# Seven products of quarters for the input projection of a hybrid state-space and attention layer

## The chip, the cores and the metric

The kernel runs on one core of one Trainium2 chip. The metric is the device time of one execution in microseconds; less is better.

## The reference

One transformer-like layer, in float32, over 1024 tokens of a prompt and 64 tokens of a second sequence that has a past of 512 tokens and stored states. Cut to what matters:

```python
xn = _rmsnorm(x, p['norm_mix_w'])
proj = xn @ p['w_in']                     # 1024 x 9248
z, xbc, dt_raw, q, k, v, gate_ssm, gate_att = jnp.split(proj, ...)   # 2048, 3072, 32, 1024, 1024, 1024, 1024, 1024
xbc_c = jax.nn.silu(causal_dwconv(conv_past, xbc, ...))              # 4 taps
y_ssm = rmsnorm_by_group(ssd_scan(...) * jax.nn.silu(z))             # 4 groups of 8 heads
q = _partial_rope(_rmsnorm(q, p['q_norm_w']), q_pos)                 # 16 heads of 64
k = _partial_rope(_rmsnorm(k, p['k_norm_w']), q_pos)
o = _rmsnorm(_diff_attention(q, k_all, v_all, q_pos, k_pos, lam))    # softmax 0 - lam * softmax 1, chunked mask
mix = sigmoid(gate_ssm) * (y_ssm @ p['w_branch_ssm']) + sigmoid(gate_att) * (o @ p['w_branch_attn'])
x = x + mix @ p['w_out']
h = _rmsnorm(x, p['norm_ffn_w']) @ p['w_up']
x = x + (silu(conv3(ha)) * hb) @ p['w_down']
```

## The kernel before

All 1088 tokens lie along the free dimension (T = 1088, HT = 544 is a half). Features lie on the 128 partitions, so the 1024 inputs are KT = 8 tiles. Every float32 operand is split into a high part, rounded to the format in which TensorE multiplies (written fp32r in the profile's rows), and the rest, its low part; `product` multiplies high by high, high by low and low by high, three matmuls a tile of the contraction.

`project(block, evac)` makes one 128-column block of w_in: it loads and splits the block (`weights`, L150 to L152: a DMA, a ScalarE copy, a VectorE subtraction), then runs 8 x 3 matmuls for each of the three column chunks of WIDE = 384, 384, 320 tokens (L158 to L160) and hands each to `evac`.

The stages, in the order of time:
- The first two quarters of the values, from plain rows while the norm's roots are computed (`plain_rows`, `token_roots`, `values`).
- `heads` for q, and for k: eight blocks each, squares, the norm, the rotation of a part, and the split rows written to q_st and k_st. The other two quarters of the values lie between (`values(2, ...)`, `values(3, ...)`).
- Attention: 8 heads of 9 units (`attend`), a unit being 128 queries. A unit's first half makes two score tiles, their maxima, exponentials and the difference of both; its second half transposes the difference and multiplies with the values. The loop runs the second half of a unit after the first half of the next one. After each unit, `fill(ATT_STEPS)` takes 1.66 steps of a stream of `project` chunks: 16 blocks z, 24 convolution blocks, 16 gate blocks (ORDER). 17 steps stand ahead (FIRST).
- The scan of the state-space part, beside it the rest of the stream and two of three `branch` products (1.5 steps at each yield), then the third branch.
- `output`, then the up projection and the down projection, both by seven products: `left_parts` makes the seven left operands from the four quarters of a pair of weight blocks, B and `right_parts` hold the right ones, and `pair`, `down_pair` run 7 x 2 steps, each 4 x 3 matmuls of QW = 272 columns (L1227, L1390), and add up the quadrants.

The names in the rows: xn is the normed input, w_hi, w_lo and wh split weights, sc the scores, p_t the exponentials, a_t and po the transposed differences and the output of a unit, pt their PSUM tile, cc and pre the convolution's rows, ye (L871) the state's products.

The order of instructions on each engine is that of the program, with `high_priority` moving loads and evacuations up, settled by a planner that gives each a due time. PSUM has eight banks: `acc` goes round the banks of `pm` and of a stage's own pool (`more`).

Of the kernel before, what the change touches and what calls it, by code (L numbers as in the profile page):

```python
# [17 lines left out]
P = 128  # L18
# [5 lines left out]
WIDE = ((0, 384), (384, 384), (768, 320))  # L24
EPS = 1e-6
# [22 lines left out]
QR = 10  # L48
QSQ = 1
# [3 lines left out]
XR = 5  # L53
ROOTS = ((0, 1), (1, 3), (3, 6), (6, 9))
QUICK = 400
AT = 4
AHEAD_IN = 100
# [3 lines left out]
FIRST = 17  # L61
ATT_STEPS = 1.66
# [4 lines left out]
def group(g):  # L67
    return 16 + g, 20 + g, *range(4 * g, 4 * g + 4)


ORDER = (("g", (15, 14)), ("z", range(4)), ("c", group(0)), ("g", range(13, 7, -1)), ("c", group(1)), ("c", group(2)),
         ("z", range(4, 8)), ("c", group(3)), ("z", range(8, 16)), ("g", range(7, 1, -1)))

# [7 lines left out]
def hybrid_layer(ctx: ExitStack, tc: tile.TileContext, xT, xt, prm, cst, rope, wvd, win, wbs, wba, wout, wup, wdn,  # L81
# [12 lines left out]
    q_st, k_st = (scratch(n, [2 * D, T]) for n in ("q_st", "k_st"))  # L94
    c_st = scratch("c_st", [2 * D, PAST])
    m_sc, n_sc = scratch("m_sc", [D, T]), scratch("n_sc", [D, T])
# [30 lines left out]
    xn_pool = tc.alloc_tile_pool(name="xn", bufs=1, side="right")  # L127

    def rows_by_part(name):

        return [[xn_pool.tile([P, KT, w], R32, name=f"{name}_{u}{x}", tag=f"{u}{x}") for u in ("hi", "lo")]
                for x, (c, w) in enumerate(WIDE)]

    xn = rows_by_part("xn")
# [26 lines left out]

    def project(block, evac):
        w_hi, w_lo = weights(block, KT, P)
        for (c, w), (hi, lo) in zip(WIDE, xn):
            ps = acc(w)
            product(ps, [(w_hi[:, k], w_lo[:, k], hi[:, k], lo[:, k]) for k in range(KT)])
            with tc.high_priority(quick or ahead):
                evac(ps, c, w)
            yield

    def branch(stage, side, src, wts, gates, adds, out, step=1):

        parts = rows_by_part("b")
# [10 lines left out]
        if gates is not None and not adds:  # L184
            ready = {(m, c): next_to(m, c, w) for c, w in WIDE for m in TURNS[0]}
        for (c, w), (hi, lo) in zip(WIDE, parts):
            for k in range(0, KT, step):
                if stage is None:
                    for u, t in enumerate((hi, lo)):
                        load(out=t[:, k : k + step].bitcast(F32),  # L190
                             in_=src[D * u + P * k : D * u + P * (k + step), c : c + w].rearrange("(k p) t -> p k t", p=P))
                else:
                    t = stage()[:, :w]
                    load(out=t, in_=src[P * k : P * (k + 1), c : c + w])
                    S.copy(hi[:, k], t)
                    V.tensor_tensor(out=lo[:, k], in0=t, in1=hi[:, k], op=ALU.subtract)
        for ms in TURNS:
            wt = [weights(wts[m], KT, P) for m in ms]
            for (c, w), (hi, lo) in zip(WIDE, parts):
                for m, (w_hi, w_lo) in zip(ms, wt):  # L200
# [5 lines left out]
                    product(ps, [(w_hi[:, k], w_lo[:, k], hi[:, k], lo[:, k]) for k in range(KT)])  # L206
# [11 lines left out]
                    yield  # L218
# [22 lines left out]
    conv_o = dq.tile([P, CONV_TILES, 6], F32, name="conv_o")  # L241

# [6 lines left out]
    def stat(w):  # L249
        t = ps1.tile([P, 512], F32, name="st", tag="st", bufs=3)  # L250
        return t[:, :w]

    st = tc.alloc_tile_pool(name="st", bufs=1, side="right")
# [3 lines left out]
    nx = tc.alloc_tile_pool(name="nx", bufs=1)  # L257
# [6 lines left out]
    def plain_rows():  # L264
        c = 0
        for x, w in enumerate(NORM):
            xc = nx.tile([P, KT, max(NORM)], F32, name="xc", tag="xc", bufs=3)
# [28 lines left out]
    def value_weights(f):  # L296
        return [weights(win[B_V + 2 * f - 4 + u], 4, 256) for u in range(2)]

    def values(f, w2, dt=None):
        m = 256 if dt is None else 272  # L300
        for i in range(9):
# [3 lines left out]
            product(ps, [(hi[:, k], lo[:, k],  # L305
                          w2[k // 4][0][:, k % 4], w2[k // 4][1][:, k % 4]) for k in range(KT)])
            vo = staged("vo")[:, :256]
            with tc.high_priority(quick or ahead):
                if dt is None:
                    S.copy(vo[:n], ps[:, :256])  # L310
                else:
                    act(vo[:n], ps[:, :256], AF.Copy, scale=rtok[:n, i : i + 1])
# [21 lines left out]
    two = [values(0, [t[1:] for t in w2], dtw)]  # L334
# [8 lines left out]
    two.append(values(1, [weights(wvd[2 + u], 4, 272, p) for u, p in enumerate((extra, first))], dtw))  # L343
# [3 lines left out]
    for i in range(8):  # L347
        for u in two:
            next(u, None)
        if i == 3:  # L350
# [3 lines left out]
            for a, b, by in ((O_CW, O_SN, 0.5), (O_SN, O_D, -0.5), (O_QN, O_FW, -1.0)):  # L354
                V.tensor_scalar_mul(par[:, a:b], par[:, a:b], by)
# [5 lines left out]
    more = s1.enter_context(tc.tile_pool(name="psx", bufs=3, space=PSUM)), 3  # L361
    nx.release()
    first.release()
    extra.release()
    extra = None

    with tc.tile_pool(name="qk", bufs=1) as qk:
        rp = qk.tile([P, 2, T], F32, name="rp")
        load(out=rp, in_=rope)
        wq8 = qk.tile([P, 8], F32, name="wq8")  # L370
        V.tensor_scalar_mul(wq8, par[:, O_QN : O_QN + 8], 0.125)

        def row(name, w=T):
            t = qk.tile([P, T], F32, name=name, tag="qr", bufs=QR)
            return t[:, :w]


        rrow = qk.tile([P, T], F32, name="rrow")
        ps = stat(P)
        PE.matmul(ps[:9], rtok, ident, start=True, stop=True)  # L380
        rt = qk.tile([9, P], F32, name="rt")
        S.copy(rt, ps[:9])
        load(out=r_sc, in_=rt)
        load(out=rrow, in_=r_sc.rearrange("a b -> (a b)")[:T].unsqueeze(0).to_broadcast([P, T]))

        def rooted_rows():

            parts = rows_by_part("xn")
            for (c, w), (hi, lo) in zip(WIDE, parts):
                for k in range(KT):  # L390
                    x = qk.tile([P, 384], F32, name="xr", tag="xr", bufs=XR)[:, :w]
                    load(out=x, in_=xT[:, k, c : c + w])
                    V.tensor_tensor(out=x, in0=x, in1=rrow[:, c : c + w], op=ALU.mult)
                    act(hi[:, k], x, AF.Copy, scale=col(O_MIX + k))
                    V.scalar_tensor_tensor(lo[:, k], x, col(O_MIX + k), hi[:, k], ALU.mult, ALU.subtract)
            return parts

        def split_out(src, j, n, to):
            hi = qk.tile([P, T], R32, name="qh", tag="qh", bufs=2)[:, :n]
            lo = qk.tile([P, T], R32, name="ql", tag="ql", bufs=2)[:, :n]  # L400
            S.copy(hi, src)
            V.tensor_tensor(out=lo, in0=src, in1=hi, op=ALU.subtract)
            for u, t in enumerate((hi, lo)):
                load(out=to[D * u + P * j : D * u + P * (j + 1), :], in_=t.bitcast(F32))

        def heads(blk0, wcol, to, plain, root=None):
            nonlocal ahead
            ss = row("ss")
            rows = [row("qr") for _ in range(KT)]

            def block(j):
                r = rows[j]

                def evac(ps, c, w):
                    S.copy(r[:, c : c + w], ps)
                    if j == 0:
# [14 lines left out]
            for _ in WIDE:  # L431
                for u in tiles[KT - 2 :]:
                    next(u)
# [1137 lines left out]
```

## Time and profile before

| | us |
|---|---|
| median of 3 runs | 2448.9 (2448.25 to 2450.0) |
| the profiled execution | 2450.28 |
| its span in the trace | 2448.5 |
| TensorE busy | 2413.0 |
| VectorE busy | 1606.9 |
| ScalarE busy | 1166.9 |
| GpSimd busy | 584.3 |

A matmul's busy time in the profile overlaps that of the next one, so busy TensorE says that it had work, and the distance of matmul starts says at what rate. The weight load ahead of each matmul has rows of its own, named PEld. Rows of groups have: line, engine, operation, output and inputs, shapes, count | busy us, mean ns of one | idle time of the engine before them and what ended it. Rows of the timeline have: start us, duration us, engine, line, operation, and a count where several of one line were merged.

### The profile page before, as it was taken

The page shows a single profiled execution, that of the slowest core. Times are in us where ns is not written, and L with a number is a line of the kernel's source. Part 1 is how long each engine was busy: PE and PEld are TensorE (multiplying, and loading weights), DVE is VectorE, ACT ScalarE, POOL GpSimd, SP SyncE. Part 2 cuts the span into 40 slices and gives each one's busy share as a digit, 9 for nine tenths or more (in the row PEclk, how much of TensorE's full clock was granted, in tenths as well). Part 3 has the DMA queues.
Part 4 walks back from the last instruction along what each step waited for, and adds up shares of the span by engine and source line. Part 5 has one row for each costly group of instructions (what it writes and reads, how often), then busy time and mean ns, then how long its engine had stood idle before and what let it go on. Part 6 is the DMA issues. An engine that isn't in the chain of part 4 may idle for free. (4 is left out here: it accounts for less than half of the span.)

```text
span 2448.5 us, 44118 instructions
## 1 busy us (share of the span) xinstructions
PE 2413.0 (99%) x16824; PEld 2334.3 (95%) x16824; DVE 1606.9 (66%) x2760; ACT 1166.9 (48%) x2517; POOL 584.3 (24%) x630
## 2 busy tenths in 40 slices
PE   8999999999999999999999999999999999998999
PEld 8999999999999999998899899999999999998999
DVE  4356366755878677538677664756977777786763
ACT  7244344644666455437655453434543343353541
POOL 0000000100111001005433341013255555535533
PEclk9999999999999999999999999999999999999999
DMA  7237368443543454264797864764124234268884
GB/s 251 94 106 258 102 247 251 146 142 109 167 142 121 131 167 125 76 208 161 256 322 259 294 218 147 224 209 154 56 91 173 91 134 163 79 240 222 203 215 79
DMA packets 245670, 418.31 MB, mean 171 GB/s; under 512 B 32137, under 2 KB 168466, under 8 KB 245330
## 3 DMA queue, kind: packets, MB, share of 16 engines
q1 hardware_dynamic: 238258, 402.40, 49.6%
q0 software_dynamic: 7200, 13.09, 3.6%
q8 instruction: 132, 2.16, 0.4%
q14 instruction: 80, 0.66, 0.1%
HBM read 277.38 MB, written 138.02 MB: 170 GB/s over the span
## 5 line engine op out<-in xcount | busy, mean ns | idle before, releaser
L158 PE MATMUL mm<-xn_hi,w_hi 128*128 128x384 f32 (+1 forms) x1408 | 471.2, 335 | 1.0 <-DVE zr L550 0.9
L160 PE MATMUL mm<-xn_hi,w_lo 128*128 128x384 f32 (+1 forms) x1408 | 467.8, 332 | 0.5 <-DVE w_lo L152 0.5
L159 PE MATMUL mm<-xn_lo,w_hi 128*128 128x384 f32 (+1 forms) x1408 | 467.1, 332 | 0.0
L158 PEld LDWEIGHTS mm<-xn_hi,w_hi 128*128 128x128 f32 x1408 | 264.7, 188 | 5.9 <-DVE zr L550 1.6
L160 PEld LDWEIGHTS mm<-xn_hi,w_lo 128*128 128x128 f32 x1408 | 264.6, 188 | 3.8 <-issue 2.0
L159 PEld LDWEIGHTS mm<-xn_lo,w_hi 128*128 128x128 f32 x1408 | 264.7, 188 | 3.0 <-issue 1.6
L152 DVE TENSOR_TENSOR w_lo<-w_f,w_hi 128x1024 fp32r<-128x1024 f32 (+1 forms) x114 | 143.6, 1260 | 111.9 <-ACT w_hi L151 109.4
L151 ACT CAST w_hi<-w_f 128x1024 fp32r<-128x1024 f32 (+1 forms) x114 | 119.6, 1050 | 113.5 <-PE mx L159 52.0
L1227 PE MATMUL mx<-n,wh 128*128 128x272 f32 x1128 | 150.5, 289 | 1.9 <-ACT wh L1042 1.2
L158 PE MATMUL mm<-b_hi,w_hi 128*128 128x384 f32 (+1 forms) x448 | 151.5, 339 | 0.9 <-ACT w_hi L151 0.5
L160 PE MATMUL mm<-b_hi,w_lo 128*128 128x384 f32 (+1 forms) x448 | 148.1, 331 | 0.3 <-DVE w_lo L152 0.3
L159 PE MATMUL mm<-b_lo,w_hi 128*128 128x384 f32 (+1 forms) x448 | 147.7, 330 | 0.1
L1227 PEld LDWEIGHTS mx<-n,wh 128*128 128x128 f32 x1128 | 144.9, 188 | 2.6 <-ACT wh L1042 1.4
L1227 PE MATMUL mx<-m,w_hi 128*128 128x272 f32 x752 | 143.8, 288 | 1.3 <-DVE hb L1263 1.1
L700 ACT ACTIVATE p_t<-sc,mx 128x1024 f32<-128x1024 f32 (+5 forms) x144 | 106.3, 741 | 80.8 <-DVE mx L691 38.3
L579 DVE SCALAR_TENSOR_TENSOR cc<-pre,par,cc 128x384 f32<-128x384 f32 (+1 forms) x216 | 125.6, 584 | 15.1 <-ACT cc L577 10.9
L1043 DVE TENSOR_TENSOR wh<-w_f,wh 128x512 fp32r<-128x512 f32 (+1 forms) x100 | 93.9, 941 | 40.9 <-ACT wh L1042 40.9
L1227 PEld LDWEIGHTS mx<-m,w_hi 128*128 128x128 f32 x752 | 118.2, 188 | 2.0 <-DVE hb L1263 1.5
L1244 POOL TENSOR_TENSOR hb<-hb,cc 128x544 f32<-128x544 f32 (+2 forms) x66 | 91.0, 1393 | 108.7 <-ACT w_hi L1042 61.1
L565 POOL MEMSET pre<- 128x3 f32 x24 | 2.4, 101 | 474.8 <-DMA z_sc<-zr 378.8
L1042 ACT CAST w_hi<-ws 128x512 fp32r<-128x512 f32 (+1 forms) x68 | 41.4, 608 | 150.3 <-PE mx L1227 82.6
L1227 PE MATMUL mx<-m,w_lo 128*128 128x272 f32 x376 | 108.3, 288 | 0.0
(418 smaller groups left out, 6513.6 us busy)
## 6 DMA issues: line engine op xcount, KB each, us to landing
w_f<-in_win_dram SPq DMA_DIRECT2D x76, 512.0 KB, 3.8
w_f<-in_wup_dram SPq DMA_DIRECT2D x45, 512.0 KB, 3.5
bc<-a_sc SPq DMA_DIRECT2D x32, 512.0 KB, 5.9
h_sc<-hb SPq DMA_DIRECT2D x44, 272.0 KB, 2.1
ht<-h_sc SPq DMA_DIRECT2D x22, 544.0 KB, 4.6
t_sc<-ht SPq DMA_DIRECT2D x22, 544.0 KB, 2.9
out_dram<-yq POOLq DMA_DIRECT2D x44, 272.0 KB, 5.6
x_sc<-cc SPq DMA_DIRECT2D x48, 192.0 KB, 2.4
```

Source lines behind the costliest of these rows:

```text
L151: S.copy(hi, w)
L152: V.tensor_tensor(out=lo, in0=w, in1=hi, op=ALU.subtract)
L158: PE.matmul(ps, a_hi, b_hi, start=i == 0, stop=False)
L159: PE.matmul(ps, a_hi, b_lo, start=False, stop=False)
L160: PE.matmul(ps, a_lo, b_hi, start=False, stop=i == n - 1)
L565: G.memset(pre[:, 0:3], 0.0)
L579: V.scalar_tensor_tensor(cc[:, :m], pre[:, i : i + m], cw(i), cc[:, :m], ALU.mult, ALU.add)
L700: act(p_t[:n, :nk], sc[c][:n, :nk], AF.Exp, bias=mx[:n, c : c + 1], accum_out=dst)
L1042: S.copy(hi, src)
L1043: V.tensor_tensor(out=lo, in0=src, in1=hi, op=ALU.subtract)
L1227: PE.matmul(ps, w[x][:, c], b[y][:, k], start=start and k == i == 0, stop=k == 3 and i == 2, skip_group_check=not start)
L1244: G.tensor_tensor(out=hb[h][:, o : o + n], in0=hb[h][:, o : o + n], in1=cc[:, d : d + n], op=ALU.mult)
```

## The change

The products for q, k, the convolution and 12 of the 16 z blocks leave `heads` and the stream and get a stage of their own, ahead of attention. It takes two blocks at a time: the pair's weights are four quarters (two halves of the contraction by two blocks), the tokens' rows four quarters (two halves of the contraction by two halves of the tokens), and seven products of quarters make the four quadrants, as the up projection does. INPUT has 26 pairs: 4 of q, 4 of k, then six times two of convolution and one of z.

- The right operands are made once. `rooted(k)` loads two rows of x, multiplies them by the norm's weight and root, forms t1 to t4, splits b11, b21 and t2 in place, and writes t3, t1, t4, b22 and b12 to scratch (p_sc); `load_part` loads and splits them before the stage, b12 at its end. The rows b11, b12, b21, b22 are then what `project` and the branches' buffers use.
- All four quarters of the values come first; `rooted` and `steps` lie beside the third and fourth.
- A half of the tokens, 544, is cut into columns of 384 and 160 (W2). `in_pair` runs, for each of seven products p and each cut s, `pile`: 4 x 3 matmuls. After each second step one left operand of the next pair is made (`left_parts`, its sums on GpSimd from the third pair on).
- The convolution is done for halves of the tokens, in `in_pair`, with the Silu function in place of a tanh and a VectorE step; z as well for these 12 blocks. Norm and rotation of q and k (`finishing`) go beside later pairs, by way of scratch (q_r, k_r); so do the cached keys.
- `project` and `branch` go over CH, four chunks of 384, 160, 384 and 160 tokens, in place of WIDE.
- The stream holds 20 blocks: 16 gates and 4 of z. `fill` counts by columns (363 are one), 0.45 a unit of attention, 4 ahead of it.
- In attention the second half of a unit runs after the first half of the second unit after it (DEEP = 2), with 5 buffers p_t for 4.

```diff
+W2, O2 = (384, 160), (0, 384)
+CH = tuple((HT * c + O2[s], W2[s]) for c in range(2) for s in range(2))
+UNIT = 363.0
+DEEP = 2
+PROBS = 5
-FIRST = 17
-ATT_STEPS = 1.66
+FIRST = 4
+ATT_STEPS = 0.45
+ORDER = (("g", (15, 14)), ("z", range(4 * ZS, 16)), ("g", range(13, 7, -1)), ("g", range(7, 1, -1)))
+INPUT = ([(k, i) for k in "qk" for i in range(4)]
+         + [x for i in range(2 * ZS) for x in (("c", 2 * i), ("c", 2 * i + 1), ("z", i))])
...
     def project(block, evac):
         w_hi, w_lo = weights(block, KT, P)
-        for (c, w), (hi, lo) in zip(WIDE, xn):
+        for (c, w), rows_of in zip(CH, plain):
...
+        def pile(key, p, s, start):
+            if start:
+                banks[key, s] = acc(W2[s])
+            ps, w, b = banks[key, s], left[n][p], parts[PARTS[p], s]
+            for k in range(4):
+                c = slice(P * k, P * (k + 1))
+                for i, (x, y) in enumerate(((0, 0), (0, 1), (1, 0))):
+                    PE.matmul(ps, w[x][:, c], b[y][:, k], start=start and k == i == 0, stop=k == 3 and i == 2,
+                              skip_group_check=not start)
+            return ps
...
+        def conv(r, c):
...
+            cc = row("fc", "cc")
+            act(cc[:, :n], pre[:, :n], AF.Identity, bias=col(O_CB + f), scale=cw(0))
+            for i in range(1, 4):
+                V.scalar_tensor_tensor(cc[:, :n], pre[:, i : i + n], cw(i), cc[:, :n], ALU.mult, ALU.add)
+            act(cc[:, :n], cc[:, :n], AF.Silu)
...
+    for n in range(1, len(INPUT)):
+        coming = in_parts(n + 1) if n + 1 < len(INPUT) else iter(())
+        u = pairs[1] if n == 1 else begun_in(n)
+        for at, (p, s) in enumerate(rest if n == 1 else [(p, s) for p in range(7) for s in range(2)]):
+            u.send((p, s))
+            if s == 1:
+                more_left(n + 1)
+            if at % 2 == 0:
+                next(beside, None)
...
+        if n in (3, 7):
+            beside = chain(beside, finishing("q" if n == 3 else "k"))
...
     def fill(rate):
         nonlocal spare
         spare += rate
-        while spare >= 1:
-            next(filler, None)
-            spare -= 1
+        while spare > 0:
+            w = next(filler, None)
+            if w is None:
+                break
+            spare -= w / UNIT
...
+                waiting.append((unit, done))
+                settle(DEEP)
                 fill(ATT_STEPS)
```

More of the change, by code (lines that the diff above doesn't have):

```diff
@@ L205, in branch @@
                     ps = acc(w)
[L206 removed]
+                    product_over(ps, w_hi, w_lo, rows_of)
                     with tc.high_priority(ahead):
@@ new lines, in hybrid_layer @@
+    making = chain(*(rooted(k) for k in range(4)))
+    for u in chain(third, fourth):
+        next(making, None)
+    run(making)
+    steps()
+    wq8 = cp.tile([P, 8], F32, name="wq8")
+    V.tensor_scalar_mul(wq8, par[:, O_QN : O_QN + 8], 0.125)
+    ahead = AHEAD
+    raw.release()
+    st.release()
+    rr.release()
+    xn_pool.release()
+    un2 = tc.alloc_tile_pool(name="xd", bufs=1)
+    rows_l = tc.alloc_tile_pool(name="rl", bufs=1)
+    rows_r = tc.alloc_tile_pool(name="rg", bufs=1, side="right")
```

671 lines of the change are left out of this document (392 added, 279 removed).

## The prediction

> **What bounds the kernel now.** I read the page's first part, then the busy time by stretch, then TensorE's timeline at three places, and last the groups by line of the engines that the change loads more.
>
> ```profile
> PE 2413.0 (99%) x16824; PEld 2334.3 (95%) x16824; DVE 1606.9 (66%) x2760; ACT 1166.9 (48%) x2517; POOL 584.3 (24%) x630
> ...
> 50.00:340.00 290.00, 288.84 (x1881) 283.75 (x1881) 136.80 (x209) 114.85 (x218) 0.00 (x0) 1.00 0.41 138
> 340.00:1080.00 740.00, 738.35 (x4732) 713.19 (x4731) 500.54 (x1060) 394.80 (x962) 48.60 (x144) 1.00 0.49 153
> ...
> 1720.00:2180.00 460.00, 456.32 (x3616) 453.80 (x3615) 349.03 (x535) 187.61 (x336) 230.05 (x251) 1.00 0.34 119
> ```
>
> In the stretch rows the columns are length, then busy time of PE, PEld (the weight loads), DVE, ACT and POOL, the granted clock, the share of the DMA engines and GB/s. TensorE is busy to 99.6% in the q, k stage (50 to 340 us), to 99.8% in attention (340 to 1080) and to 99.2% in the up projection, all at the full clock. Every other engine has room. A busy PE is not yet a PE at its peak, so the next thing to read is how far apart the matmuls start.
>
> ```profile
> 300.01 0.33 PE L159 MATMUL mm<-xn_lo,w_hi 128*128 128x384 f32 x1
> 300.19 0.33 PE L160 MATMUL mm<-xn_hi,w_lo 128*128 128x384 f32 x1
> 300.36 0.33 PE L158 MATMUL mm<-xn_hi,w_hi 128*128 128x384 f32 x1
> 300.53 0.33 PE L159 MATMUL mm<-xn_lo,w_hi 128*128 128x384 f32 x1
> ...
> 475.44 0.31 PE L160 MATMUL mm<-xn_hi,w_lo 128*128 128x320 f32 x1
> 475.59 0.31 PE L158 MATMUL mm<-xn_hi,w_hi 128*128 128x320 f32 x1
> 475.74 0.31 PE L159 MATMUL mm<-xn_lo,w_hi 128*128 128x320 f32 x1
> 475.88 0.31 PE L160 MATMUL mm<-xn_hi,w_lo 128*128 128x320 f32 x1
> 476.03 0.22 PE L686 MATMUL sc<-kh,q 128*128 128x128 f32 x1
> 476.09 0.27 PE L687 MATMUL sc<-kl,q 128*128 128x128 f32 x1
> 476.20 0.27 PE L686 MATMUL sc<-kh,q 128*128 128x128 f32 x1
> 476.31 0.55 PE L734 MATMUL po<-v_t,a_t 128*128 128x128 f32 x3
> ```
>
> Starts of 384-column matmuls are (300.53 - 300.01) / 3 = 173.3 ns apart, those of 320 columns (475.88 - 475.44) / 3 = 146.7 ns. The difference, 26.7 ns for 64 columns, is 0.417 ns a column, and leaves 13.3 ns fixed. So TensorE streams columns with nothing between, and the time of this kernel is its matmuls times their prices. What changes the time is the number and the widths of the matmuls, as long as nothing else comes late.
>
> **The price of a narrow matmul.** The change cuts 544 columns into 384 and 160. No row here has 160 columns. By columns alone it would take 160 x 0.417 + 13.3 = 80 ns. The scores above have 128 columns (by columns alone 66.7 ns): the first is followed after 0.06 us, the next ones after 0.11 us each. The second row of numbers to read is that of the weight loads, one ahead of each matmul.
>
> ```profile
> 476.03 0.19 PEld L687 LDWEIGHTS sc<-kl,q 128*128 128x128 f32 x1
> 476.14 0.19 PEld L686 LDWEIGHTS sc<-kh,q 128*128 128x128 f32 x1
> 476.25 0.53 PEld L734 LDWEIGHTS po<-v_t,a_t 128*128 128x128 f32 x4
> ...
> 1176.17 0.52 PEld L871 LDWEIGHTS ye<-in,start 128*128 128x128 f32 x4
> ...
> L158 PEld LDWEIGHTS mm<-xn_hi,w_hi 128*128 128x128 f32 x1408 | 264.7, 188 | 5.9 <-DVE zr L550 1.6
> ...
> L158 PEld LDWEIGHTS mm<-w_hi,xn_hi 128*64 128x64 f32 x16 | 2.2, 135 | 0.0
> ```
>
> Loads follow each other at 0.11 us when the matmuls between are short: 476.03 to 476.14 to 476.25; the next three steps (0.53 - 0.19) / 3 = 0.113; at 1176.17 it is (0.52 - 0.19) / 3 = 0.11, and those matmuls (the state's, L871) stream only 64 columns. A load of 128 columns lasts 188 ns, one of 64 columns 135 ns: 53 ns for 64 columns, so 106 ns for 128 besides a latency of 82 ns that overlaps. One load runs ahead of the running matmul, not two: the first narrow matmul of a run is cheap since its follower's weights came during the wide one before it. So a matmul of a run costs the longer of its columns and its load. For 384 columns that is 173.3 ns, for 160 columns the load, 106 to 113 ns; I take 111. The lower end by rows would be 80, if loads were ahead of narrow ones too; nothing here shows that.
>
> The Trainium skill, page "TensorE: Matmul & The Clock Gate", section "LDWEIGHTS (loading the stationary operand)", gives a load as its columns divided by 1.2, in ns, whatever the contraction: 107 ns for 128 columns, which speaks against narrow products, and the 188 and 135 ns above agree with its slope. The same page, section "Back-to-back issue gap", has N / 2.4 + 2.5 ns for an isolated matmul, 69 ns for 160 columns; by that figure alone, an estimate from the page, 4296 narrow matmuls would take 180 us less than by 111 ns, and it says itself that this leaves out the weight load.
>
> **The change part by part.** *Products.* Before, a 128-column block of weights takes 24 matmuls (8 tiles of the contraction, three terms) for each of 384, 384 and 320 columns: 24 x (173.3 + 173.3 + 146.7) = 11.84 us. The change takes two blocks at once by seven products of quarters: 7 x 4 x 3 = 84 matmuls for each width, 84 x (173.3 + 111) = 23.88 us a pair. 52 blocks (8 q, 8 k, 24 convolution, 12 z) become 26 pairs: 620.9 us for 615.7 us, **+5.2 us**. An eighth of the columns is saved and all of it goes into the narrow half: `pile` runs twelve matmuls of 384 columns and then twelve of 160. (With 80 ns it would be 553.2, -62.5 us.)
>
> The seven-product stage that is there already has 272-column halves:
>
> ```profile
> 2307.12 10.53 PE mx L1390 x84
> ```
>
> that is 125.4 ns each, 250.8 for 544 columns against 284.3 for 384 and 160. That is where the gain goes.
>
> *The chunks of all that stays.* `project` and `branch` now go over CH, four chunks of 384, 160, 384, 160, where WIDE had three. 20 blocks stay in the stream (4 z, 16 gates) and 24 in the three branches. Each takes 24 x 2 x 284.3 = 13.65 us in place of 11.84: +1.81 us x 44 = **+79.5 us**. (With 80 ns, +0.32 x 44 = +14.1 us.) Values, `output` and the up and down projections keep their widths.
>
> *Filler.* Before, 72 attention units took 1.66 steps each of the stream, now 0.45 in units of 363 columns (4.55 us); FIRST falls from 17 to 4. TensorE's sum does not change by that, but its cover over attention does.
>
> ```profile
> L686 PEld LDWEIGHTS sc<-kh,q x208: 133/188/193, 393.2 to 1051.7; 128*128 128x128 f32 x96, 128*64 128x64 f32 x8
> ...
> L756 PEld LDWEIGHTS pt<-con,o_t x72: 134/139/143, 485.5 to 1079.5; 128*128 128x128 f32 x64, 64*128 64x128 f32 x8
> ...
> L691 DVE TENSOR_REDUCE mx<-sc 128x1 f32<-128x1024 f32 (+4 forms) x80 | 76.7, 963 | 19.8 <-PE sc L687 18.6
> L704 DVE SCALAR_TENSOR_TENSOR p_t<-p_t,sm 128x1024 f32<-128x1024 f32 (+8 forms) x72 | 58.8, 816 | 2.0
> L152 DVE TENSOR_TENSOR w_lo<-w_f,w_hi 128x1024 fp32r<-128x1024 f32 x42 | 51.1, 1218 | 23.3 <-ACT w_hi L151 20.9 <-PE po L734 2.3
> ...
> L722 DVE COPY a_t<-pt 128x512 f32<-128x512 f32 (+3 forms) x56 | 29.7, 530 | 12.8 <-PE pt L715 12.5
> L695 DVE TENSOR_REDUCE mx<-sc 128x2 f32<-128x256 f32 (+3 forms) x32 | 26.0, 813 | 0.4
> L755 DVE SCALAR_TENSOR_TENSOR o_t<-o_t,ors,wsub 128x128 f32<-128x128 f32 (+1 forms) x72 | 19.7, 346 | 0.2
> ...
> L703 DVE SCALAR_TENSOR_TENSOR sm<-sm,nlam,s 128x1 f32<-128x1 f32 (+1 forms) x72 | 15.6, 217 | 1.9
> L760 DVE TENSOR_TENSOR ol<-pt,oh 128x512 fp32r<-128x512 f32 (+1 forms) x23 | 12.2, 536 | 6.8 <-ACT zr L549 2.7 <-DMA o_sc<-oh 2.0 <-DMA o_sc<-ol 2.0
> L702 DVE RECIPROCAL sm<-sm 128x1 f32<-128x1 f32 (+1 forms) x72 | 11.5, 159 | 25.3 <-ACT p_t L700 25.1
> ```
>
> Attention runs from its first score at 393 to its last transposes at 1080 us. Of these 686 us, 72 x 1.66 steps of 3.95 us, 472 us, are filler, so its own matmuls take some 214 us. After: 214 + 72 x 0.45 x 4.55 = 214 + 147 = 361 us. VectorE's own work there is 76.7 + 58.8 + 29.7 + 26.0 + 19.7 + 15.6 + 12.2 + 11.5 = 250 us (the smallest rows left out), and 11 blocks of filler bring 11 splits of 1.22 us, 13 us: about 0.73 of 361 us, with the small rows perhaps 0.8; in the up projection it runs at 349 / 460 = 0.76 beside a full TensorE. So VectorE should keep pace, with more small waits since less filler lies between a unit's scores and its softmax. Running the second half two units late is the cover for those: nothing new waits, it only holds one more `p_t` (5 buffers for 4). I put **+10 us** for attention, between 0 and 30.
>
> *VectorE and the others in the new stage.*
>
> ```profile
> L1238 DVE SCALAR_TENSOR_TENSOR cc<-pre,par,cc 128x546 f32<-128x546 f32 (+1 forms) x69 | 64.1, 929 | 7.4 <-ACT cc L1236 6.2
> L1043 DVE TENSOR_TENSOR wh<-w_f,wh 128x512 fp32r<-128x512 f32 x51 | 52.8, 1035 | 26.3 <-ACT wh L1042 26.3
> L1043 DVE TENSOR_TENSOR w_lo<-w_f,w_hi 128x512 fp32r<-128x512 f32 x17 | 25.6, 1507 | 0.0
> L1043 DVE TENSOR_TENSOR w_lo<-ws,w_hi 128x512 fp32r<-128x512 f32 x34 | 24.9, 733 | 1.0
> L1043 DVE TENSOR_TENSOR wh<-ws,wh 128x512 fp32r<-128x512 f32 x18 | 20.3, 1128 | 23.5 <-ACT wh L1042 23.5
> L1265 DVE TENSOR_TENSOR hb<-mx,u 128x272 f32<-128x272 f32 x25 | 11.0, 439 | 14.7 <-PE mx L1227 13.6 <-issue 1.1
> ```
>
> These are 17 pairs of the up projection. Seven weight splits a pair: 123.6 / 17 = 7.3 us. Five products added out of PSUM in two pieces, 10 x 0.44 = 4.4 us. A convolution pair adds 2 blocks x 2 halves x 3 taps of some 544 columns, 12 x 0.93 = 11.1 us. Together 22.8 us of VectorE beside 23.9 us of TensorE; a z pair has 11.7. The norms and rotations of k (`finishing`) come on top while the first four convolution pairs run, some 30 us by the same prices (twelve half rows of a scale and a split at 0.9 + 0.7 us, and four rotations), against 4 x 23.9 - (3 x 22.8 + 11.7) = 15.5 us of room: **+10 us**, between 0 and 25, since seven PSUM banks let TensorE run only a few products ahead. GpSimd and ScalarE stay far below.
>
> *Transitions.* The loads of t3, t1, t4 and b22 wait for the last value product, and stand on SP's queue ahead of the weights of the third pair; TensorE has four products of two pairs and t2's, 5 x 3.41 = 17 us, before it needs t3. The first head's loads wait for the last pair's rows behind 4 units of gates, 18 us. `rooted`'s arithmetic lies under 18 value products. DMA share was 0.41, so the added 5.6 MB each way of differences and the q and k round trip have room. **+5 us**, between -5 and +15.
>
> Sum: 5.2 + 79.5 + 10 + 10 + 5 = +110 us. The profiled execution took 2450.28 us (span 2448.5), the median of the runs is 2448.9, 1.4 us below: 2450.3 + 110 - 1.4 = **2559 us**.
>
> **The rivals.**
> *A narrow matmul costs its columns.* Then 26 pairs save 62.5 us, the chunks cost 14.1 us, and with 25 us of waits (TensorE is shorter, VectorE's room less) the time is 2449 - 48 + 25 = 2426 us. For it: the first narrow score (0.06 us). Against: each one after it, and the 64-column ones. It decides below a price of some 86 ns: 4296 narrow matmuls (26 x 84 + 44 x 48) turn 1 ns into 4.3 us, so (48 - 25) / 4.3 = 5 ns above 80 the saving and the waits cancel. The isolated gap of the Trainium skill (page and section above) would make it so; the rows of loads do not bear it out. Chance 0.12, of which 0.09 lies beyond 0.2% faster, 0.01 within and 0.02 beyond it slower; 0.2% is about what a measurement of this kernel can tell from no change.
> *VectorE becomes the bound.* If it can hold no more than the 0.76 it has in the up projection, convolution pairs take 22.8 / 0.76 = 30 us, 12 x 6.1 = +73 us, and attention (250 + 13 + some 25 of small rows) / 0.76 = 379, +18 us: 2449 + 85 + 91 + 5 = 2630 us. Against it: in the up projection VectorE waits, it isn't the one waited for. Chance 0.17.
> *Under 256 columns the stream runs at half rate.* 128 columns in 111 ns are also two times 128 columns. Then 160 cost 2 x 160 x 0.417 + 5 = 138 ns (5 as 111 ns has over 2 x 128 x 0.417), +27 x 4.3 = +116: 2675 us. Against it: the first narrow score's 0.06 us. Chance 0.05.
>
> **How the numbers follow.** The forecast has 0.66. Its own range: at 106 ns, without waits, 2449 + 63 = 2512; at 113 with all upper waits (+70) 2449 + 93 + 70 = 2612. To hold 8 in 10 the range goes from 2515 to 2660, which takes in the VectorE case and leaves out the first rival and the third. Slower 0.66 + 0.17 + 0.05 + 0.02 = 0.90, same 0.01, faster 0.09.
>
> **What would show it.** In the timeline of the new stage, twelve 160-column matmuls start 111 ns apart and their weight loads too; 80 ns would be the first rival, 138 the third. The new stage lasts about 630 us, a gate block 13.6 us, attention about 370 us. VectorE as the bound would show as TensorE's idle time ended by VectorE, above some 60 us in the convolution pairs. A stall at the start of the new stage ended by a DMA into t3 or by a split would be a transition mis-sized. A time below 2500 us makes the price of the narrow matmul wrong.

## The result and the profile after

| | before | after |
|---|---|---|
| median of the runs, us | 2448.8 (2448.25 to 2450.0) | 2704.0 (2702.8 to 2708.4) |
| span of the profiled execution, us | 2448.5 | 2701.0 |
| TensorE busy, us | 2413.0 | 2568.8 |
| TensorE idle (span less busy), us | 35.5 | 132.2 |

After to before is 1.1045, with an interval of 1.1026 to 1.1064. The change costs 255 us where +110 was forecast, and the time is 44 us above the end of the range. The page of after has, in its first two parts:

```profile
PE 2568.8 (95%) x18504; PEld 2471.7 (92%) x18504; DVE 1785.9 (66%) x3080; ACT 1230.3 (46%) x2623; POOL 720.6 (27%) x702
...
PEclk9999998999999999888999999989999999999999
```

There are 18504 - 16824 = 1680 more matmuls, and that is exact: 26 x 168 - 52 x 72 = 624 in the pairs and 44 x 24 = 1056 in the chunks. The price is read in TensorE's timeline of the new stage (L600 is `pile` in `in_pair`):

```profile
610.36 0.51 PE L600 MATMUL mx<-t,w_hi 128*128 128x384 f32 x2
610.71 0.34 PE L600 MATMUL mx<-t,w_lo 128*128 128x384 f32 x1
610.88 0.35 PE L600 MATMUL mx<-t,w_hi 128*128 128x160 f32 x2
611.06 0.28 PE L600 MATMUL mx<-t,w_lo 128*128 128x160 f32 x1
...
611.40 0.27 PE L600 MATMUL mx<-t,w_lo 128*128 128x160 f32 x1
...
612.07 0.28 PE L600 MATMUL mx<-t,w_lo 128*128 128x160 f32 x1
```

From 611.06 to 612.07 lie nine starts of 160 columns: 112 ns each. The two of 384 columns from 610.36 to 610.71 take 175 ns each. Over the whole of 600 to 790 us, where TensorE never waits (row below), 1327 matmuls take 190.00 us: 286.4 ns for a wide and a narrow one, where 284.3 was put down. So the products cost nearly what the prediction put down, 94 us at this distance for 5.2 + 79.5 = 85. The other 168 us of the span are TensorE waiting (132.2 - 35.5 = 97 us more idle) and TensorE working slower than its price (2568.8 - 2413.0 - 85 = 71 us; 9 of them are these 2 ns a pair, and most of the rest is the halved clock of the last section). Where, the busy time by stretch tells (columns as in the prediction):

```profile
100.00:150.00 50.00, 39.08 (x265) 35.75 (x265) 38.77 (x63) 22.85 (x46) 0.00 (x0) 0.83 0.68 233
300.00:530.00 230.00, 201.82 (x1287) 196.68 (x1286) 170.63 (x286) 90.18 (x162) 62.07 (x72) 0.93 0.53 179
600.00:790.00 190.00, 190.00 (x1327) 190.00 (x1326) 133.52 (x215) 78.47 (x138) 61.48 (x90) 1.00 0.25 88
820.00:1100.00 280.00, 278.50 (x1965) 265.31 (x1964) 158.08 (x362) 134.94 (x374) 0.00 (x0) 1.00 0.51 156
1100.00:1240.00 140.00, 106.67 (x610) 88.21 (x608) 104.56 (x274) 83.76 (x246) 0.00 (x0) 0.84 0.44 132
1700.00:1800.00 100.00, 88.74 (x554) 82.13 (x554) 59.39 (x117) 43.88 (x99) 18.80 (x10) 0.90 0.52 158
```

TensorE has gaps in three kinds of place, and in each the granted clock falls too: while the new stage begins and k is finished beside its pairs (100 to 150, 300 to 530), in the second half of attention (1100 to 1240), and in the scan and its end (1700 to 1800). Between them (600 to 790, 820 to 1100) it is as full as before. No engine is full in the gaps: VectorE is at 0.74 to 0.78 in the first three stretches with gaps and at 0.70 in 600 to 790, where TensorE never waits.

To put a number on each stage I added up its matmuls, each at its distance of starts at full clock (173.3, 146.7, 126.7, 111 ns for 384, 320, 272, 160 columns, and so on for the small ones), and took the sum from the stage's length. What is left, us (with 384 and 160 columns it holds the 9 us by which their pair is dearer):

| lost in | before | after | e1_272 | e8_pace | e6_cover | e10_all |
|---|---|---|---|---|---|---|
| start to first score (new stage with it) | 17 | 77 | 96 | 56 | 85 | 52 |
| attention | 17 | 79 | 78 | 80 | 55 | 65 |
| scan to output | 5 | 47 | 40 | 39 | 45 | 62 |
| up and down | 18 | 21 | 23 | 21 | 18 | 20 |
| sum | 57 | 224 | 237 | 196 | 203 | 199 |

So the 168 us are +60, +62, +42 and +3. In the four runs below that leave the new stage untouched, its row is 84 to 88, against 77 in after; differences up to 10 us in it say nothing. What ended TensorE's waits in after, and VectorE's in 300 to 530 us (engine, line, releaser: us in total, times, longest):

```profile
PE sc L916 <- ACT p_t L930: 24.4, 17, 3.9
PE mm L600 <- DVE u L673: 8.5, 3, 4.4
PE mm L157 <- DVE w_lo L149: 8.1, 5, 3.5
PE mm L155 <- DVE b_g L223: 7.3, 4, 4.3
PE mx L600 <- DVE u L671: 7.1, 4, 3.4
PE mx L600 <- DVE pre L682: 6.5, 3, 3.1
```

```profile
DVE x L712 <- DMA x<-k_r: 18.3, 9, 3.8
...
DVE pre L682 <- DMA k_st<-x: 3.9, 3, 2.3
```

In attention a score waits for the exponentials that free its bank (L930). In the convolution pairs TensorE waits for VectorE, which evacuates PSUM (L671, L673, L682). But VectorE itself is held: next in its order stands a step of k's norm (L712), whose row of k has not landed yet, and an evacuation that could run stands behind it. One such place, on VectorE and on TensorE:

```profile
420.47 0.79 DVE L712 SCALAR_TENSOR_TENSOR x<-x,par,ss 128x544 f32<-128x544 f32 x1 [2.39 <-DMA x<-k_r]
421.17 0.32 DVE L671 TENSOR_TENSOR u<-mm,u 128x160 f32<-128x160 f32 x1
```

```profile
421.55 1.57 PE L600 MATMUL mm<-t,wh 128*128 128x160 f32 x12 [1.84 <-DVE u L671]
```

And the row that the evacuation writes (L682) is at times one that still goes out to k_st.

### The profile page after: what moved, and what is told of

It is laid out like the page before. It is cut to its first block, busy times and chain, and to the rows that moved or that the text cites. A ratio compares the mean times of both kernels' runs of the same rounds, so it can differ in the third digit from the quotient of the medians.

```text
span 2701.0 us, 48417 instructions
## 1 busy us (share of the span) xinstructions
PE 2568.8 (95%) x18504; PEld 2471.7 (92%) x18504; DVE 1785.9 (66%) x3080; ACT 1230.3 (46%) x2623; POOL 720.6 (27%) x702
## 5 line engine op out<-in xcount | busy, mean ns | idle before, releaser
L155 PE MATMUL mm<-b,w_hi 128*128 128x160 f32 (+1 forms) x1152 | 364.1, 317 | 12.4 <-DVE b_g L223 7.3
L157 PE MATMUL mm<-b,w_lo 128*128 128x160 f32 (+1 forms) x1152 | 361.0, 314 | 8.1 <-DVE w_lo L149 8.1
L156 PE MATMUL mm<-b,w_hi 128*128 128x160 f32 (+1 forms) x1152 | 360.5, 313 | 0.0
L155 PEld LDWEIGHTS mm<-b,w_hi 128*128 128x128 f32 x1152 | 223.8, 194 | 18.9 <-DVE b_g L223 6.2
L157 PEld LDWEIGHTS mm<-b,w_lo 128*128 128x128 f32 x1152 | 223.9, 194 | 12.1 <-DVE w_lo L149 10.1
L156 PEld LDWEIGHTS mm<-b,w_hi 128*128 128x128 f32 x1152 | 224.1, 195 | 3.2 <-issue 2.3
L600 PE MATMUL mx<-t,wh 128*128 128x384 f32 (+1 forms) x840 | 133.2, 313 | 9.5 <-DVE u L671 7.1
L600 PE MATMUL mx<-t,w_hi 128*128 128x160 f32 (+1 forms) x608 | 132.3, 310 | 7.2 <-ACT pre L680 3.9
L600 PEld LDWEIGHTS mx<-t,wh 128*128 128x128 f32 x840 | 127.2, 194 | 11.1 <-DVE u L671 8.8
L930 ACT ACTIVATE p_t<-sc,mx 128x1024 f32<-128x1024 f32 (+5 forms) x144 | 106.1, 740 | 60.5 <-DVE p_t L934 24.7
L600 PE MATMUL mx<-b,wh 128*128 128x384 f32 (+1 forms) x840 | 131.8, 311 | 0.6 <-ACT u L669 0.6
L630 DVE SCALAR_TENSOR_TENSOR cc<-pre,par,cc 128x544 f32<-128x544 f32 (+1 forms) x144 | 128.4, 916 | 4.3 <-ACT cc L628 4.0
L600 PEld LDWEIGHTS mx<-b,wh 128*128 128x128 f32 x840 | 126.0, 192 | 1.7 <-ACT u L669 0.9
```

The costliest lines, as they stand in the source:

```text
L155: PE.matmul(ps, a_hi, b_hi, start=i == 0, stop=False)
L156: PE.matmul(ps, a_hi, b_lo, start=False, stop=False)
L157: PE.matmul(ps, a_lo, b_hi, start=False, stop=i == n - 1)
L600: PE.matmul(ps, w[x][:, c], b[y][:, k], start=start and k == i == 0, stop=k == 3 and i == 2, skip_group_check=not start)
L630: V.scalar_tensor_tensor(cc[:, :n], pre[:, i : i + n], cw(i), cc[:, :n], ALU.mult, ALU.add)
L930: act(p_t[:n, :nk], sc[c][:n, :nk], AF.Exp, bias=mx[:n, c : c + 1], accum_out=dst)
```

## The experiments

The main theory after the result: the price is right, and what was mis-sized is waits, for want of work that covers them. Rivals: the narrow price is worse than seen, VectorE is the bound, or one step at a transition holds all.

**The price alone (e1_272).** Halves of 272 and 272 columns.

```diff
-W2, O2 = (384, 160), (0, 384)
+W2, O2 = (272, 272), (0, 272)
```

> The change with halves cut into 272 and 272 columns in place of 384 and 160 (W2, O2, and the place of the fourth quarter's value weights); the same columns, the same number of matmuls. Theory: a 160-column matmul costs its weight load, 111 ns, so 4296 pairs of 384 and 160 go from 284.3 to 250.8 ns: -144 us, 2704 to some 2560 us, if the waits stay; TensorE's shorter products leave VectorE less room, so up to 30 us of it may come back as waits, 2560 to 2590. Rival (the waits, not the widths, carry the loss, since VectorE or the buffers set the pace of the new stage and of attention): the time falls by less than 60 us.

Measured: 2582.9 us, ratio 1.0547 (1.0530 to 1.0565), 121 us less than the change. In the timeline:

```profile
630.00 0.28 PE L596 MATMUL mx<-t,w_lo 128*128 128x272 f32 x1
...
630.38 0.29 PE L596 MATMUL mx<-t,w_lo 128*128 128x272 f32 x1
...
634.92 0.29 PE L596 MATMUL mx<-b,w_lo 128*128 128x272 f32 x1
```

One such row stands at every third matmul, so 39 starts lie between 630.00 and 634.92: 126 ns. The 26 x 84 + 44 x 48 = 4296 pairs of a wide and a narrow matmul save 286.4 - 252.3 = 34 ns each, 147 us. TensorE's busy time fell by just that (2422.1 against 2568.8 us), its idle time rose by 26 us (157.9 against 132.2), and 121 us is what came. The narrow price is shown, and so is that waits don't shrink with it: the kernel is still 5.5% slower than before.

**The new stage's start (e2_steps).** In 107 to 140 us the first pair waits for raw rows and for the small matmuls of the steps' sums. Here the steps are traced ahead of the rows.

```diff
+    steps()
     making = chain(*(rooted(k) for k in range(4)))
...
     run(making)
-    steps()
```

> The change with the time steps' chain (steps) traced ahead of the rooted rows instead of after them. Theory: TensorE's idle time at 107 to 140 us is the chain's five small matmuls standing in TensorE's queue ahead of the first pair and waiting for VectorE one after another (15 us lost there, some of it at a cold clock); with the chain beside the third quarter of the values it goes: -12 to -16 us. Rival (the first pair would wait anyway, for t3 or its weights): less than -4 us, with idle time at the same place ended by another release.

Measured: 2704.0 us (ratio 1.1035, 1.1019 to 1.1052), no change; TensorE is busy for 22.4 of the 34 us from 107 to 141, against 23.1 in after. The rival holds. The first pair's matmuls wait for its evacuation on ScalarE (L669), now 9.4 us at once where it was 3.5. In after that evacuation waits 7.3 us for a row that still goes out from the steps (a_sc<-af); here it stands behind splits that wait 5.1 us for loads into t. This loss of some 15 us stays without a tested cure.

**k's finishing beside the pairs (e3_zfirst, e8_pace, e11_apart).** First, four z pairs, with half of VectorE's work of a convolution pair, straight behind k:

```diff
-         + [x for i in range(2 * ZS) for x in (("c", 2 * i), ("c", 2 * i + 1), ("z", i))])
+         + [("z", i) for i in range(4)] + [("c", i) for i in range(3)] + [("z", 4)] + [("c", i) for i in range(3, 6)] + [("z", 5)]
+         + [("c", i) for i in range(6, 12)])
```

> The change with the order of the pairs altered: four z pairs follow the k pairs, and the convolution pairs come after them (two z pairs among them). Theory: the 47 us lost between 300 and 530 us are the norms and rotations of k sharing rows (four fp, three fc) and VectorE's queue with the convolution; beside z pairs, which hold a row for a shorter time and have 12 us of VectorE a pair less, they go: -25 to -45 us. Rival (convolution pairs are bound by VectorE by themselves, 22.8 us of 23.9): the loss stays, spread over the convolution pairs, less than -10 us.

Measured: 2688.7 us, ratio 1.0968 (1.0950 to 1.0987): 15 us gained, between the theory's 25 to 45 and the rival's less than 10. Waits for k's rows remain on VectorE beside the z pairs (in 300 to 500 us 5.8 us for k_r, 8.5 us for rows that go out to k_st). So VectorE's load is not all of it; then the finishing slower, from the ninth pair on:

```diff
-            if at % 2 == 0:
+            if at % (2 if n < 8 else 6) == 0:
                 next(beside, None)
```

> From the ninth pair of the new stage on, the finishing of k (norms and rotations) and of the stage's rows beside the pairs is advanced at every sixth step of a pair instead of every second. Theory (the finishing takes row buffers and VectorE's place in the queue ahead of the pairs' own steps): the stage's loss falls from 68 to about 50 us, 2684 to 2696 us. Rival (the finishing's rows have to come back before attention anyway, and go late into the stage's end): the loss moves to the stage's end or the attention's first head, 2700 to 2720 us.

Measured: 2678.7 us, ratio 1.0943 (1.0912 to 1.0974), 25 us less, more than the theory's 8 to 20; the first head does not come later. The stretch that held most of the gaps:

```profile
300.00:530.00 230.00, 220.87 (x1489) 219.24 (x1488) 188.93 (x306) 108.33 (x189) 70.42 (x88) 0.97 0.54 182
```

VectorE is busier in it than in after, 0.82 for 0.74, and TensorE waits for 9 us where it waited for 28. And the finishing not beside the pairs at all:

```diff
-        if n in (3, 7):
-            beside = chain(beside, finishing("q" if n == 3 else "k"))
-    run(beside)
+        if n == 3:
+            beside = chain(beside, finishing("q"))
+    run(chain(beside, finishing("k")))
```

> The finishing of k (norms and rotations) is taken from beside the pairs and run alone after the last of them. Theory (it is this finishing, by its rows and its steps in VectorE's queue, that makes the convolution pairs wait): the pairs' loss between 300 and 780 us falls from about 50 to under 12 us, and the finishing then stands bare behind the pairs, some 60 to 90 us with TensorE idle: 2715 to 2755 us in all. Rival (the convolution pairs wait by their own steps and rows): the loss in 300 to 780 us stays above 30 us, and the finishing is added on top: 2760 us or more.

Measured: 2751.9 us, ratio 1.1223 (1.1195 to 1.1250), inside the theory's range. Stretches and TensorE's wait in 780 to 860 us:

```profile
300.00:350.00 50.00, 45.79 (x286) 45.32 (x285) 43.09 (x73) 18.85 (x36) 11.54 (x9) 0.90 0.60 200
350.00:780.00 430.00, 430.00 (x2999) 429.74 (x2998) 295.97 (x470) 179.44 (x314) 130.92 (x185) 1.00 0.27 93
790.00:850.00 60.00, 0.10 (x1) 0.00 (x0) 27.32 (x44) 11.77 (x18) 0.00 (x0) 0.51 0.81 271
```

```profile
PE sc L916 <- DMA kh<-k_st: 65.4, 1, 65.4
```

From 350 us on the same pairs run with TensorE at 430.00 of 430 us, the full clock and VectorE at 0.69. They don't wait by their own work: neither VectorE nor the seven banks bind the pairs alone. What makes them wait in after is the finishing of k. It lasts 65 us alone, and in it VectorE is busy for only 27 of 60 us, with the DMA engines at 0.81: it is a chain through DRAM (row in, scale, split, rows out), not VectorE's work. In after it was packed into about 230 us of the pairs; at a third of that pace it costs 25 us less.

**Attention (e4_deep1, e5_held, e6_cover, e12_cover75).** The last transposes of the eight heads stand at 911, 979, 1050, 1108, 1149, 1192, 1232 and 1277 us: heads with filler take 58 to 70 us, the later ones 40 to 45. TensorE's own work for a head is some 27 us (214 / 8 of the prediction), so a bare head loses some 16 us. The planner's order had drawn the filler forward. First, the second halves one unit late as before the change:

```diff
-DEEP = 2
-PROBS = 5
+DEEP = 1
+PROBS = 4
```

> Attention's second halves one unit late as before the change (DEEP 1, PROBS 4), all else as in the changed kernel. Theory: attention waits for want of cover, and the late halves are what keeps part of the chain of softmax steps covered; without them attention grows by 10 to 40 us: 2714 to 2744 us. Rival: holding two units back keeps score rows and a bank taken and is itself the wait; then attention shrinks by 10 us or more: below 2694 us. Within 5 us of 2704: the two late halves are worth nothing either way.

Measured: 2711.4 us, ratio 1.1060 (1.1044 to 1.1077). That is 7 us more than the change, under the theory's 10, and the two ratios' intervals overlap: the late halves help little, if at all. Next, filler held to its own head: its weights' loads are issued after the previous head's output row is stored.

```diff
-            load(out=w, in_=block.rearrange("p (k m) -> p k m", k=k))
+            if hold is not None:
+                with tc.issue_after(hold.ins):
+                    load(out=w, in_=block.rearrange("p (k m) -> p k m", k=k))
...
-                    load(out=o_sc[D * u + P * h : D * u + P * (h + 1), b0 * P : b0 * P + w], in_=t.bitcast(F32))
+                    hold = load(out=o_sc[D * u + P * h : D * u + P * (h + 1), b0 * P : b0 * P + w], in_=t.bitcast(F32))
```

> The change with the loads of the filler's weight blocks in attention queued behind the last stored output rows of the head before, so that the filler can't run more than about a head ahead. Theory: the order that was planned took the filler of all eight heads in the first five (no filler product runs between 1100 and 1240 us, where a head takes 41 us of which TensorE works 25); spread out, attention takes some 375 in place of 425 us: -30 to -60 us. Rival (a head takes its chain of softmax steps anyway, 41 us and more, with filler or without): every head takes 50 us and more, and the time changes by less than 15 us either way.

Measured: 2730.9 us, ratio 1.1146 (1.1129 to 1.1162): 27 us slower; attention loses 109 us. My theory that spreading the filler evenly would cover all heads fell. A head with an even share (179 / 8 = 22 us; the expectation of e6_cover counts 179 us of filler in attention) takes 50 to 66 us; it loses some 14 us (109 / 8), nearly what a bare one loses. Then more filler in attention, taken from the scan:

```diff
-ATT_STEPS = 0.45
-SCAN_STEPS = 1.5
-BRANCH_AT = 4
+ATT_STEPS = 0.65
+SCAN_STEPS = 1.15
+BRANCH_AT = 2
```

> More of the stream of z blocks is given to each attention unit (0.65 for 0.45 units of filler), less to each scan step (1.15 for 1.5), and the first two branches are let in from the scan's third span on instead of its fifth. Some 14 units of filler, about 70 us by the 179 us that 36 units hold in attention now, move from the scan to attention. Theory (the work that can cover waits is what is short in attention, and the scan has some to spare until its end): attention's loss falls from 79 to about 40 us, the scan's stays at 40 to 60: 2655 to 2680 us. Rival (the scan needs its cover as much): what attention gains the scan loses, 2695 to 2715 us. Rival (attention's heads take a set time by their own chain whatever lies beside): attention's loss falls but only because its stage holds more work, and the scan, now bound by its own chain, gives back less than 72 us: 2680 to 2700 us.

Measured: 2677.6 us, ratio 1.0929 (1.0892 to 1.0966), 26 us less, within the theory's range, though attention's loss falls to 55 and not to 40. In attention:

```profile
830.00:1200.00 370.00, 368.12 (x2597) 352.10 (x2596) 205.54 (x473) 178.82 (x484) 0.00 (x0) 1.00 0.50 153
1200.00:1329.00 129.00, 109.69 (x697) 96.40 (x695) 82.85 (x212) 71.71 (x217) 0.00 (x0) 0.89 0.37 118
```

Five heads are now full, three are bare. One step further (0.75, 0.95, from the second span on):

> As e6_cover, further: 0.75 units of filler for each attention unit, 0.95 for each scan step, the branches from the scan's second span on. Some 7 more units, about 36 us of work, go from the scan to attention. Theory (a head with its full share of about 45 us of filler hardly waits, a bare head waits 16 us): a sixth head is covered, attention's loss falls from 55 to about 40 us, the scan's stays near 45: 2655 to 2670 us. Rival (the scan now lacks the cover): the scan's loss rises by as much or more: 2678 to 2700 us.

Measured: 2688.6 us, ratio 1.0976 (1.0959 to 1.0993):

```profile
830.00:1260.00 430.00, 425.01 (x2996) 405.27 (x2994) 237.71 (x550) 207.59 (x568) 0.00 (x0) 1.00 0.52 158
1260.00:1338.00 78.00, 63.97 (x400) 52.77 (x398) 54.16 (x139) 45.98 (x139) 0.00 (x0) 0.87 0.35 112
```

Attention's loss falls only from 55 to 50, and the scan's rises from 45 to 51: the rival's range holds here, though the two runs' intervals touch. The two stages together lose 126, 100 and 101 us in after, e6_cover and e12_cover75, and 22 before the change. Sharing out what is left gets back 26 of the 104. For attention the rest fits the work that is no longer there to share: before, the stream held 36 blocks more (12 z and 24 convolution, 36 x 11.84 = 426 us). No run put such work back, and none tells whether the chain's length or the banks of the scores (L930) hold a bare head.

**All together (e9_best, e10_all, e10b_all).** e9 joins the edits of e1_272, e3_zfirst and e6_cover; e10_all adds e8_pace's; e10b_all is e1_272 and e8_pace with the filler of e12_cover75 and the change's order of pairs.

> Together: products of 272 and 272 columns instead of 384 and 160, four z pairs straight behind k, and the filler spread of e6_cover. If the parts add up: 2704 less 121 (columns), less 15 (z first), less 30 (cover): about 2540 us, range 2520 to 2575. It would then still be over 70 us above the kernel before; the theory that the change loses by price alone would have it at about 2470.

> The edits of e9_best and that of e8_pace together: products of 272 and 272 columns, four z pairs behind k, more filler in attention, and k's finishing advanced at every sixth step from the ninth pair on. If e8_pace's 25 us come from the same waits as the z pairs' 15 (row buffers of the finishing), little is left to gain over e9_best's 2563: 2545 to 2560 us. If they are two separate waits: 2535 to 2545 us. Even this one stays some 90 us above the kernel before.

> As e10_all, but with the z pairs between the convolution pairs where the change has them, and still more filler in attention (0.75 per unit, 0.95 per scan step, branches from the scan's second span on). If cover is what attention lacks and the scan has some to spare, this comes out below e10_all by about 10 us: 2530 to 2545 us; if the scan has none to spare it comes out above by as much: 2550 to 2570 us.

Measured: e9_best 2562.7 us, inside its range (ratio 1.0453, 1.0435 to 1.0471), e10_all 2541.8 (1.0376, 1.0361 to 1.0392), e10b_all 2557.3 (1.0445, 1.0422 to 1.0469). The pace adds 21 us to the z pairs' gain, so these are mostly two separate waits by the expectation's own measure. e10b_all loses 14 us more in the new stage than e10_all (its z pairs are not first) and 9 more in the scan, and 12 less in attention: sharing differently only moves the waits. The best of them is 92 us slower than the kernel before. With 272 columns the products are cheaper than before by some 54 us (26 x (168 x 0.126 - 23.68) = -65, 44 x (96 x 0.126 - 11.84) = +11), so its waits, with the half rate behind them, still come to nearly 150. No version of the change that was run beats the kernel before.

## Why the prediction was wrong

*Price of a narrow matmul, right.* 111 ns was put down and 112 measured; the two rivals by other prices (80 and 138 ns) fall with the timeline, and e1_272 shows the price in the time of the whole kernel.

*Products +5.2 and chunks +79.5, right*, by the count of matmuls, and within 9 us (94 for 85) by their distances. They make a third of the loss.

*"I put +10 us for attention, between 0 and 30": measured +62.* This is the step that failed most. The prediction compared VectorE's sum of work with the stage's length (0.8) and took the rest as slack: "nothing new waits". Attention's unit is a chain (scores, maximum, exponentials, difference, transposes, values) that passes from engine to engine. In 1100 to 1240 TensorE is at 0.76, VectorE at 0.75, ScalarE at 0.60, none full. A bare head takes 40 to 45 us by this chain, whatever the shares. The filler had filled TensorE meanwhile, 59 us a head, and the prediction itself counted that it would fall to 18. The late halves are worth 7 us at most, not the cover that it took them for.

*k's finishing +10 (0 to 25) and transitions +5 (-5 to 15): together measured +60.* Some 15 lie at the start of the stage (100 to 150 us): in after not the load into t3 that the prediction named, but the steps' small matmuls and the first pair's evacuation (L669), whose row comes free late; with the steps moved, loads into t took their place. Most of the rest lies in 300 to 530 us, beside the finishing; that the finishing is its cause is what e11_apart shows. The step summed VectorE's work against its room. The finishing uses VectorE for less than half of its time, and what the rows of waits show is rows that wait for a DMA at the head of VectorE's queue, and row buffers shared with the pairs. How much of the loss is these waits and how much VectorE's load while both run packed is not shown: in e11_apart the pairs take 295.97 us of VectorE for 2999 matmuls, so an estimate for the 1287 of 300 to 530 us in after is 127 of the 170.63 us there, and some 44 for the finishing, where the prediction put 30. Against 184 us of matmuls (1287 x 143.2 ns), 171 us are a share of 0.93, with little room left.

*The scan: not in the sum at all; measured +42.* That the stage would wait more had no term. Its cause stays open. It is not want of work in sum: by the table's prices the matmuls of this stage come to some 645 us after and 635 before, and e6_cover moved about 70 us of them to attention while the loss went from 47 to 45. TensorE waits for the splits of the filler's weights (8.1 us, L149) and, where the scan goes over into the third branch, for what evacuates it and for its operands (7.3 us, L223, and 3.0 us, L205); no run moved these.

*A term for the granted clock: none was put down.* TensorE at half rate behind its waits costs some 51 us (last section), which are part of the losses of these three places.

*The rival that VectorE becomes the bound* gave 2630 us with waits in the convolution pairs and in attention. It named the right places, but its ceiling of 0.76 is not one: in e8_pace VectorE is busy for 0.82 of 300 to 530 us beside TensorE at 0.96, and where it is at 0.69 to 0.70 the pairs run without a wait. The sign of it that the prediction named, TensorE's idle time ended by VectorE above some 60 us in the convolution pairs, was not reached. What ended it before L600's matmuls in after (us, times):

```profile
  DVE u L671: 8.9, 5
  DVE u L673: 8.5, 3
  DVE pre L682: 7.1, 4
```

That is 24.5 us, and the cause of part of it is the finishing again.

*Gate block 13.6 us, new stage about 630, attention about 370*: a gate block's 48 pairs take 13.7 us at 286.4 ns, the stage lasted 702 us and attention 458.

## What to carry to other kernels

A narrow matmul's price can be read ahead from the distance of weight loads in the trace, and summed by count. When a change takes filler away from beside a chain, the shares of the engines do not price it: take the time of the chain without cover, less the bound engine's own work, times the units that go bare (here four heads by 16 us, 64 us, where 62 were lost), and put down a term for every later stage whose order changes. Work run "beside" another is not free because its engine has room: a step that waits for its DMA holds up everything behind it on that engine, and the same steps at a third of the pace cost 25 us less. Add to each wait the half rate that can follow it.

## What the runs showed of the hardware

Gaps cost more than their length. In e11_apart TensorE waited 65 us, and 6 once more behind it. The stretch after that and its timeline:

```profile
870.00:872.00 2.00, 2.00 (x8) 2.00 (x7) 0.00 (x0) 0.00 (x0) 0.00 (x0) 0.50 0.80 237
```

```profile
869.62 0.52 PE L155 MATMUL mm<-b,w_hi 128*128 128x384 f32 x1
869.94 0.52 PE L156 MATMUL mm<-b,w_hi 128*128 128x384 f32 x1
...
872.82 0.52 PE L156 MATMUL mm<-b,w_hi 128*128 128x384 f32 x1
873.14 0.38 PE L157 MATMUL mm<-b,w_lo 128*128 128x384 f32 x1
873.36 0.34 PE L155 MATMUL mm<-b,w_hi 128*128 128x384 f32 x1
873.54 0.33 PE L156 MATMUL mm<-b,w_hi 128*128 128x384 f32 x1
```

Eleven matmuls start 320 ns apart, (873.14 - 869.62) / 11, then they go over to 173 to 180: after a long gap TensorE runs at half rate for some 4 us. The Trainium skill, page "TensorE: Matmul & The Clock Gate", section "Part 1: The HAM clock gate", says that the clock halves after an idle window of about 3.4 us, returns after about as long of sustained work, and that starts are N / 1.2 ns apart while it is halved, 320 ns for 384 columns. The trace agrees on the return (3.5 us of starts at 320 ns) and on the distance. On the gap it does not: shorter ones are enough here. In after, behind a single wait of 1.99 us:

```profile
1345.13 0.45 PE L1085 MATMUL cb<-con,in 128*128 128x128 f32 x1 [1.99 <-ACT b_cb L1088]
...
1347.65 0.41 PE L157 MATMUL mm<-b,w_lo 128*128 128x160 f32 x1
...
1348.50 0.34 PE L155 MATMUL mm<-b,w_hi 128*128 128x160 f32 x1
1348.68 0.27 PE L156 MATMUL mm<-b,w_hi 128*128 128x160 f32 x1
```

Four starts of 160 columns lie between 1347.65 and 1348.50: 212 ns each, where they take 112 at the full clock. The granted clock is 0.50 from 1345.20 to 1348.61 us. The length of the wait alone does not decide: in before a wait of 2.98 us that ends at 2198.11 us left the clock at 1.00.

This tells what made TensorE's busy time longer than its price. In after the granted clock is 0.50 in 22 stretches of 3.4 to 17 us, each begun during or just behind waits of TensorE, and at the very end. All of them together, with the busy time of each engine:

```profile
sum 137.22, PE 109.77 PEld 99.79 DVE 98.53 ACT 47.94 POOL 15.63; mean PE 4.77 PEld 4.34 DVE 4.28 ACT 2.08 POOL 0.68
```

TensorE works for 110 us at half rate, and for 7 us in before. Half of the difference, an estimate of 51 us, is most of the 71 us. So a wait costs more than its idle time, here 97 us of idle time and some 51 us behind it. The prediction had no term for it.
